# Matmul with rotary embedding: tiles in pairs over three PSUM banks, and part of the transposes on VectorE

## The chip, the cores and the metric

The kernel runs on one core of a Trainium2 chip. The metric is device time in microseconds, from launch to end of the slowest (here the only) core. Before the change five runs took 166.57 to 167.12 us, with a median of 166.95 us. A profile comes from one execution; times inside it count from its first instruction.

## The reference

`x` is 16 x 512 x 768, the weight 768 x 768, all float32; there are 12 heads of 64 columns. The product is rotated by halves of a head, with tables that depend on the row of the sequence:

```python
y = np.matmul(x, weight).reshape(batch, seq, n_heads, head_dim)
y1, y2 = y[..., :32], y[..., 32:]
out1 = y1 * cos1 - y2 * sin1
out2 = y2 * cos2 + y1 * sin2
out = concatenate([out1, out2])
```

## The kernel before, in words

The 8192 rows of `x` are 64 tiles of 128 rows. Row `4p + r` of a batch lies on partition `p` of tile `r`, so that each partition of a tile is a run of 3072 bytes in memory, and so that tile `i` needs the tables' part `i % 4`. A tile goes through these steps:

1. `load` (L75): SP's queue brings the tile to SBUF as float32 (393 KB).
2. `cast` (L86): ScalarE rounds it to float16.
3. `transpose` (L89): TensorE transposes six 128 x 128 blocks against an identity matrix into one PSUM bank (L93), and ScalarE copies them to SBUF (`xT`).
4. `mm` (L97, L103): for each of six blocks of the contraction, two matmuls, 512 and 256 columns wide, accumulate in a two-bank PSUM tile `psy`. The transposed tile is the operand that TensorE loads as weights; the weight matrix streams.
5. `rope` (L111): VectorE multiplies the product by the cosines (`tv`, L116) and, with the halves of each head swapped, by the signed sines (`qv`, L122), both out of PSUM; GpSimd adds the two (L130).
6. `store` (L136): a DMA issued from ScalarE's queue writes the tile.

The order on each engine is the order of the source, as the schedule is written by hand. In the main loop, iteration `i` loads tile `i + 5`, transposes tile `i + 1`, casts tile `i + 2`, multiplies tile `i`, rotates it, and stores tile `i - 3`. Eleven buffers hold loaded tiles, three PSUM tiles of two banks the products, and two banks the transposed blocks.

At the start the six row blocks of the weight arrive as 393 KB loads between the first tiles of `x`, VectorE rounds each (L83), and three tiles are multiplied block by block as they come. Matmuls on a zeroed tile (L141) keep TensorE busy before. The last tile is multiplied in two halves of 384 columns, each of which VectorE rotates and adds, and SP stores.

DMA issues wait in their engine's order like any other instruction: a load that waits for a buffer holds up SP alone, a store that waits holds up ScalarE's casts and copies behind it.

Of the kernel before, what the change touches and what calls it, by code (L numbers as in the profile page):

```python
# [10 lines left out]
FP32 = mybir.dt.float32  # L11
FP16 = mybir.dt.float16
MULT = mybir.AluOpType.mult
ADD = mybir.AluOpType.add


@with_exitstack
def kernel(
    ctx: ExitStack,
    tc: tile.TileContext,  # L20
    x: bass.AP,
    weight: bass.AP,
    cos: bass.AP,
    sin: bass.AP,
    n_heads: int,
    out: bass.AP,
):
    nc = tc.nc
    P = nc.NUM_PARTITIONS

    B, S, H = x.shape
    NH = int(n_heads)
    D = H // NH
    HD = D // 2
    NKT = H // P
    NMB = B * S // P
    SB = S // P
    NSPLIT = [(0, 512), (512, H - 512)]
    HALVES = [(0, H // 2), (H // 2, H // 2)]
    FIRST = 3  # L40
    AHEAD = 8


    xv = x.rearrange("b (p r) h -> b r p h", r=SB)
    ov_dram = out.rearrange("b (p r) h -> b r p h", r=SB)

    konst = ctx.enter_context(tc.tile_pool(name="konst", bufs=1))
    ident = konst.tile([P, P], FP16)
    cos_sb = konst.tile([P, SB, D], FP32)
    tee_sb = konst.tile([P, SB, D], FP32)  # L50
    w_raw = konst.tile([P, NKT, H], FP32)
    w_sb = konst.tile([P, NKT, H], FP16)

    xpool = ctx.enter_context(tc.tile_pool(name="xpool", bufs=AHEAD + 3))
    cpool = ctx.enter_context(tc.tile_pool(name="cpool", bufs=4))
    tpool = ctx.enter_context(tc.tile_pool(name="tpool", bufs=FIRST + 2))
    rpool = ctx.enter_context(tc.tile_pool(name="rpool", bufs=4))
    opool = ctx.enter_context(tc.tile_pool(name="opool", bufs=5))
    pt_pool = ctx.enter_context(tc.tile_pool(name="pt", bufs=2, space=bass.MemoryType.PSUM))
    py_pool = ctx.enter_context(tc.tile_pool(name="py", bufs=3, space=bass.MemoryType.PSUM))  # L60

    cold = konst.tile([P, 512], FP16)
    cold_ps = pt_pool.tile([P, 512], FP32, tag="pt", name="cold_ps")

    xss, x16, xTT, psys, ovs = {}, {}, {}, {}, {}

    def copy(eng, o, i_):
        if eng is nc.scalar:
            eng.copy(out=o, in_=i_)  # L69
        else:  # L70
            eng.tensor_copy(out=o, in_=i_)  # L71

    def load(i):
        xss[i] = xpool.tile([P, H], FP32, tag="xs", name="xs")
        nc.sync.dma_start(out=xss[i], in_=xv[i // SB, i % SB])  # L75

    wv = weight.rearrange("(kt p) n -> p kt n", p=P)

    def load_w(kt):
        nc.sync.dma_start(out=w_raw[:, kt], in_=wv[:, kt])  # L80

    def cast_w(kt):
        nc.vector.tensor_copy(out=w_sb[:, kt], in_=w_raw[:, kt])  # L83

    def cast(i, eng):
        x16[i] = cpool.tile([P, H], FP16, tag="xc", name="xc")  # L86
        copy(eng, x16[i], xss.pop(i))

    def transpose(i, eng):  # L89
        xc = x16.pop(i)  # L90
        pt = pt_pool.tile([P, NKT, P], FP16, tag="pt", name="pt")
        for kt in range(NKT):
            nc.tensor.transpose(pt[:, kt, :], xc[:, ts(kt, P)], ident)  # L93
        xTT[i] = tpool.tile([P, NKT, P], FP16, tag="xT", name="xT")
        copy(eng, xTT[i], pt)

    def mm(i, kt, parts=NSPLIT):  # L97
        if i not in psys:
            psys[i] = py_pool.tile([P, 2, 512], FP32, tag="psy", name="psy").rearrange(
                "p b n -> p (b n)"  # L100
            )
        for noff, nsz in parts:
            nc.tensor.matmul(  # L103
                psys[i][:, ds(noff, nsz)],
                xTT[i][:, kt, :],
                w_sb[:, kt, ds(noff % H, nsz)],
                start=(kt == 0),
                stop=(kt == NKT - 1),
            )

    def rope(i, c0, n, ps, add_eng):  # L111
        sb = i % SB
        nh = n // D
        tv = rpool.tile([P, H], FP32, tag="tv", name="tv")[:, :n]
        qv = rpool.tile([P, H], FP32, tag="qv", name="qv")[:, :n]
        nc.vector.tensor_tensor(  # L116
            out=tv.rearrange("p (h d) -> p h d", d=D),
            in0=ps.rearrange("p (h d) -> p h d", d=D),
            in1=cos_sb[:, sb, :].unsqueeze(1).broadcast_to((P, nh, D)),
            op=MULT,  # L120
        )
        nc.vector.tensor_tensor(  # L122
            out=qv.rearrange("p (h t d) -> p h t d", t=2, d=HD),
            in0=ps.rearrange("p (h t d) -> p h t d", t=2, d=HD)[:, :, ::-1, :],
            in1=tee_sb[:, sb, :].rearrange("p (t d) -> p t d", t=2)
            .unsqueeze(1).broadcast_to((P, nh, 2, HD)),
            op=MULT,
        )
        ov = ovs[i]
        add_eng.tensor_tensor(out=ov[:, ds(c0, n)], in0=tv, in1=qv, op=ADD)  # L130

    def rope_whole(i):
        ovs[i] = opool.tile([P, H], FP32, tag="ov", name="ov")
        rope(i, 0, H, psys.pop(i)[:, 0:H], nc.gpsimd)

    def store(i):  # L136
        nc.scalar.dma_start(out=ov_dram[i // SB, i % SB], in_=ovs.pop(i))

    def warm(n):
        for _ in range(n):  # L140
            nc.tensor.matmul(cold_ps, cold[:, 0:P], cold, start=True, stop=True)  # L141

    ctx.enter_context(tc.manual_schedule())

    id_dram = nc.inline_tensor(np.eye(P, dtype=np.float16), name="identity")
    nc.vector.memset(cold, 0.0)  # L146
    nc.scalar.dma_start(out=ident, in_=id_dram.ap())
    load(0)
    load_w(0)
    load_w(1)  # L150
    load(1)
    nc.scalar.dma_start(out=cos_sb, in_=cos.rearrange("(p r) d -> p r d", r=SB))
    nc.scalar.dma_start(out=tee_sb, in_=sin.rearrange("(p r) d -> p r d", r=SB))
    load_w(2)
    load_w(3)
    load(2)
    load_w(4)
    load_w(5)
    for i in range(FIRST, AHEAD):
        load(i)  # L160

    warm(9)
    cast(0, nc.vector)
    transpose(0, nc.vector)
    warm(4)
    for kt in (0, 1):
        cast_w(kt)
        mm(0, kt)
    cast(1, nc.scalar)
    transpose(1, nc.scalar)  # L170
    mm(1, 0)
    mm(1, 1)
    for kt in (2, 3):
        cast_w(kt)
        mm(0, kt)
        mm(1, kt)
    cast(2, nc.scalar)
    transpose(2, nc.scalar)
    for kt in range(4):
        mm(2, kt)  # L180
    cast_w(4)
    for i in range(FIRST):
        mm(i, 4)
    cast_w(5)
    nc.vector.tensor_scalar_mul(  # L185
        out=tee_sb[:, :, 0:HD], in0=tee_sb[:, :, 0:HD], scalar1=-1.0
    )
    cast(3, nc.scalar)
    mm(0, 5)
    rope_whole(0)  # L190
    mm(1, 5)
    rope_whole(1)
    transpose(3, nc.scalar)
    cast(4, nc.scalar)
    mm(2, 5)
    rope_whole(2)

    for i in range(FIRST, NMB):
        if i + AHEAD - FIRST < NMB:
            load(i + AHEAD - FIRST)  # L200
        if i + 1 < NMB:
            transpose(i + 1, nc.scalar)
        if 4 < i + 2 < NMB:
            cast(i + 2, nc.scalar)
        if i < NMB - 1:
            for kt in range(NKT):
                mm(i, kt)
            rope_whole(i)
            store(i - 3)
    i = NMB - 1  # L210
    ovs[i] = opool.tile([P, H], FP32, tag="ov", name="ov")
    for n, (c0, sz) in enumerate(HALVES):
        for kt in range(NKT):
            if i not in psys:
                psys[i] = py_pool.tile([P, 2, 512], FP32, tag="psy", name="psy")
            nc.tensor.matmul(  # L216
                psys[i][:, n, 0:sz],
                xTT[i][:, kt, :],
                w_sb[:, kt, ds(c0, sz)],
                start=(kt == 0),  # L220
                stop=(kt == NKT - 1),
            )
    for j in range(NMB - 4, NMB - 1):
        store(j)
    for n, (c0, sz) in enumerate(HALVES):
        rope(i, c0, sz, psys[i][:, n, 0:sz], nc.vector)
        nc.sync.dma_start(out=ov_dram[i // SB, i % SB, :, ds(c0, sz)], in_=ovs[i][:, ds(c0, sz)])


# [33 lines left out]
```

## Time and profile before

| | |
|---|---|
| median of 5 runs | 166.95 us (166.57 to 167.12) |
| the profiled execution | 166.57 us, its span 164.8 us |
| TensorE clock granted | 0.995 of full, on average |
| TensorE matmul busy | 152.6 us, 93% of the span |
| VectorE busy | 123.0 us, 75% |
| GpSimd busy | 114.5 us, 69% |
| ScalarE busy | 98.0 us, 59% |
| moved by DMA | 53.19 MB, mean 323 GB/s |

A line of the groups reads: source line, engine, operation, what it writes and reads, shape, count; then busy time in us and the mean of one in ns; then the engine's idle time ahead of such instructions and what ended it. A line of the waits reads: who waited for whom, us in total, how often, longest. A line of the chain reads: start, length, what. Rows of 40 digits or rates cut the span into equal slices. A matmul's own mean (ns) overlaps its neighbours; the pieces of the chain give the pace.

### The profile page before, as it was taken

How to read it: one execution, taken by the hardware profiler on the slowest of the kernel's cores; microseconds unless marked ns; L12 is line 12 of the kernel's file. 1: busy time of each engine (PE TensorE's matmuls, PEld its weight loads, DVE VectorE, ACT ScalarE, POOL GpSimd, SP SyncE). 2: the span in 40 equal slices, each digit the busy share in tenths (PEclk: the TensorE clock that was granted, in tenths of full speed). 3: DMA queues.
4: the chain of work that ended last, by engine and by line, in shares of the span. 5: the costliest groups of instructions: out<-in, count | busy, mean ns of one | idle time of the engine just before them, and what ended most of it. 6: DMA issues, size and time to landing. Idle time of an engine off the chain costs nothing.

```text
span 164.8 us, 3136 instructions
## 1 busy us (share of the span) xinstructions
PE 152.6 (93%) x1165; PEld 98.3 (60%) x1165; DVE 123.0 (75%) x142; ACT 98.0 (59%) x127; POOL 114.5 (69%) x67
## 2 busy tenths in 40 slices
PE   7967699999999999999999999999999999999930
PEld 2334466666666666666666666666666666666610
DVE  0532997788777787778877788777787777877792
ACT  3053666676666776667766677666776667766400
POOL 0000598778877788777887778877788777887760
PEclk9999999999999999999999999999999999999997
DMA  4999999999999999999999999999999974334535
GB/s 150 406 403 400 403 401 415 397 413 399 350 339 341 343 356 351 335 343 339 350 345 336 372 343 346 335 356 348 325 373 324 345 278 195 148 154 178 227 157 191
DMA packets 19887, 53.19 MB, mean 323 GB/s; under 512 B 2336, under 2 KB 2848, under 8 KB 19872
## 3 DMA queue, kind: packets, MB, share of 16 engines
q1 hardware_dynamic: 10368, 27.92, 49.0%
q10 hardware_dynamic: 9504, 25.07, 38.2%
q8 instruction: 9, 0.15, 0.4%
q14 instruction: 6, 0.05, 0.1%
HBM read 27.82 MB, written 25.17 MB: 322 GB/s over the span
## 4 chain that ended last, share of the span: by engine, by line
PE 88%; DMA 4%; ACT 2%; DVE 2%; issue 1%; SPq 1%; DVEq 0%
PE psy L103 74%; PE pt L93 13%; DMA xs<-in_x_dram 4%; PE psy L216 1%; DVE ov L130 1%; ACT xc L69 1%; ACT xT L69 1%; DVE qv L122 1%; SPq L80 1%; DVE tv L116 0%; SPq L75 0%; DVEq L130 0%; DVEq L116 0%
## 5 line engine op out<-in xcount | busy, mean ns | idle before, releaser
L130 POOL TENSOR_TENSOR ov<-tv,qv 128x768 f32<-128x768 f32 x63 | 114.3, 1817 | 45.1 <-DVE qv L122 43.5
L103 PE MATMUL psy<-w_sb,xT 128*128 128x512 f16 x756 | 133.5, 326 | 2.0 <-ACT xT L69 1.8
L103 PEld LDWEIGHTS <-xT 128*128 128x128 f16 x756 | 71.2, 98 | 43.5 <-ACT xT L69 2.1
L116 DVE TENSOR_TENSOR tv<-psy,cos_sb 128x768 f32<-128x768 f32 (+1 forms) x65 | 61.4, 945 | 29.9 <-PE psy L103 28.8
L69 ACT COPY xT<-pt 128x768 f16<-128x768 f16 x63 | 50.3, 798 | 49.2 <-PE pt L93 49.2
L122 DVE TENSOR_TENSOR qv<-psy,tee_sb 128x768 f32<-128x768 f32 (+1 forms) x65 | 60.8, 935 | 0.0
L69 ACT CAST xc<-xs 128x768 f16<-128x768 f32 x63 | 52.6, 836 | 5.6 <-DMA xs<-in_x_dram 5.6
L93 PE MATMUL pt<-ident,xc 128*128 128x128 f16 x384 | 32.2, 221 | 2.2 <-ACT xc L69 2.2
L93 PEld LDWEIGHTS <-xc 128*128 128x128 f16 x384 | 26.9, 99 | 11.5 <-ACT xc L69 2.9
L141 PE MATMUL cold_ps<-cold 128*128 128x512 f16 x13 | 5.3, 570 | 1.2 <-DVE cold L146 1.2
L83 DVE CAST w_sb<-w_raw 128x768 f16<-128x768 f32 x6 | 3.3, 558 | 3.8 <-DMA w_raw<-in_weight_dram 3.7
L141 PEld LDWEIGHTS <-cold 128*128 128x128 f16 x13 | 1.6, 136 | 3.5 <-issue 2.2
L71 DVE CAST xc<-xs 128x768 f16<-128x768 f32 x1 | 0.6, 559 | 3.2 <-DMA xs<-in_x_dram 3.2
L69 ACT ACT_TABLE_LOAD x1 | 1.3, 1283 | 2.1 <-issue 2.1
L216 PE MATMUL psy<-w_sb,xT 128*128 128x384 f16 x12 | 2.1, 326 | 0.0
L130 DVE TENSOR_TENSOR ov<-tv,qv 128x384 f32<-128x384 f32 x2 | 1.7, 862 | 0.1
L216 PEld LDWEIGHTS <-xT 128*128 128x128 f16 x12 | 1.2, 98 | 0.8
L71 DVE COPY xT<-pt 128x768 f16<-128x768 f16 x1 | 0.6, 557 | 0.9 <-PE pt L93 0.9
L146 DVE MEMSET cold<- 128x256 uint32 x1 | 0.3, 272 | 0.9 <-PEq L244 0.9
L244 POOL MEMSET const-float32-0.0<- 128x1 f32 x1 | 0.1, 98 | 0.2 <-issue 0.2
L185 DVE TENSOR_SCALAR tee_sb<-tee_sb 128x128 f32<-128x128 f32 x1 | 0.2, 220 | 0.0
L244 POOL MEMSET const-bfloat16-1.0<- 128x1 bf16 x1 | 0.1, 101 | 0.0
(2 smaller groups left out, 0.2 us busy)
## 6 DMA issues: line engine op xcount, KB each, us to landing
xs<-in_x_dram SPq DMA_DIRECT2D x64, 384.0 KB, 5.7
out_dram<-ov ACTq DMA_DIRECT2D x63, 384.0 KB, 4.9
w_raw<-in_weight_dram SPq DMA_DIRECT2D x6, 384.0 KB, 5.8
out_dram<-ov SPq DMA_DIRECT2D x2, 192.0 KB, 2.2
cos_sb<-in_cos_dram ACTq DMA_DIRECT2D x1, 128.0 KB, 4.7
tee_sb<-in_sin_dram ACTq DMA_DIRECT2D x1, 128.0 KB, 5.8
ident<-identity ACTq DMA_DIRECT2D x1, 32.0 KB, 3.1
```

The lines of the kernel that those rows point to most:

```text
L69: eng.copy(out=o, in_=i_)
L71: eng.tensor_copy(out=o, in_=i_)
L80: nc.sync.dma_start(out=w_raw[:, kt], in_=wv[:, kt])
L83: nc.vector.tensor_copy(out=w_sb[:, kt], in_=w_raw[:, kt])
L93: nc.tensor.transpose(pt[:, kt, :], xc[:, ts(kt, P)], ident)
L103: nc.tensor.matmul(psys[i][:, ds(noff, nsz)], xTT[i][:, kt, :], w_sb[:, kt, ds(noff % H, nsz)], start=(kt == 0), stop=(kt == NKT - 1),)
L116: nc.vector.tensor_tensor(out=tv.rearrange("p (h d) -> p h d", d=D), in0=ps.rearrange("p (h d) -> p h d", d=D), in1=cos_sb[:, sb, :].unsqu ...
L122: nc.vector.tensor_tensor(out=qv.rearrange("p (h t d) -> p h t d", t=2, d=HD), in0=ps.rearrange("p (h t d) -> p h t d", t=2, d=HD)[:, :, : ...
L130: add_eng.tensor_tensor(out=ov[:, ds(c0, n)], in0=tv, in1=qv, op=ADD)
L141: nc.tensor.matmul(cold_ps, cold[:, 0:P], cold, start=True, stop=True)
L146: nc.vector.memset(cold, 0.0)
L216: nc.tensor.matmul(psys[i][:, n, 0:sz], xTT[i][:, kt, :], w_sb[:, kt, ds(c0, sz)], start=(kt == 0), stop=(kt == NKT - 1),)
```

## The change

Tiles are handled in 32 pairs: the two tiles of pair `n` are the same part `r = n % 4` of two neighbouring batches, and so share the tables.

- **PSUM.** A pair's product lies in one tile of three banks, 1536 columns without a gap; there are two such tiles in place of three of two banks. The first tile's 768 columns are written as 512 and 256, the second's as 256 and 512. In pairs 0 and 1, where tiles are multiplied in turns, a matmul of zeros first opens the middle bank.
- **Rotation.** One VectorE multiplication takes the pair twice, once by the cosines and once by the sines with their sign and place prepared (`csn`); the swap of halves moves into GpSimd's addition, which takes 1536 columns in one instruction. A store writes a pair (786 KB).
- **Transposes.** From pair 8 on the second tile of a pair isn't transposed by TensorE. VectorE transposes 32 x 32 blocks of 4-byte words, each holding two neighbouring float16 columns. That leaves blocks in their place, so the load arranges them: four loads of 98 KB, each to 32 partitions in runs of 768 bytes, two on SP's queue and two on ScalarE's, four pairs ahead, with five buffers.
- **Column order.** A word holds two columns, so the contraction is cut as `t, e` (three parts by even and odd columns) for all tiles, and the weight's rows are loaded to match. Casts gather pairs of columns; the loads of weights on TensorE read every second float16.
- **Start.** Four tiles of `x` are loaded before the weight, the tables after it, all on SP's queue. Two tiles are multiplied with each weight block as it comes, a third one block behind.
- **End.** The six tiles of the last three pairs are multiplied into PSUM tiles of their own and rotated in two pieces each. The last tile's pieces are added by VectorE, the others by GpSimd.

```diff
-    py_pool = ctx.enter_context(tc.tile_pool(name="py", bufs=3, space=bass.MemoryType.PSUM))
+    FIRST = 8
+    AHEAD = 8
+    AHEAD_B = 4
+    ALONE = 3
+    def by_blocks(n, s):
+        return n >= FIRST and s == 1
+    xpool = ctx.enter_context(tc.tile_pool(name="xpool", bufs=FIRST + AHEAD))
+    bpool = ctx.enter_context(tc.tile_pool(name="bpool", bufs=AHEAD_B + 1))
+    rpool = ctx.enter_context(tc.tile_pool(name="rpool", bufs=3))
+    opool = ctx.enter_context(tc.tile_pool(name="opool", bufs=4))
+    py_pool = ctx.enter_context(tc.tile_pool(name="py", bufs=2, space=bass.MemoryType.PSUM))
...
+    def load_blocks(n):
+        if n >= NP or not by_blocks(n, 1):
+            return
+        b, r = where(n, 1)
+        xss[n, 1] = bpool.tile([P, H], FP32, tag="xb", name="xb")
+        src = x[b].rearrange("(j a r) (q k) -> r q a j k", r=SB, a=R, q=NQ)
+        dst = xss[n, 1].rearrange("p (j k) -> p j k", j=NQ)
+        for q in (0, 2, 1, 3):
+            eng = nc.sync if q < 2 else nc.scalar
+            eng.dma_start(out=dst[ts(q, R)], in_=src[r, q])
...
+    def cast(n, s, eng):
...
+        if by_blocks(n, s):
+            src = src.rearrange("p (j a t e) -> p t (j a) e", j=NQ, t=NT, e=2)
+        else:
+            src = src.rearrange("p (m t e) -> p t m e", t=NT, e=2)
+        copy(eng, xc.rearrange("p (t m e) -> p t m e", t=NT, e=2), src)
+    def transpose(n, s, eng):
+        xc = x16.pop((n, s)).rearrange("p (t m e) -> p t e m", t=NT, e=2)
+        pt = pt_pool.tile([P, NT, 2, P], FP16, tag="pt", name="pt")
+        for t, e in CHUNKS:
+            nc.tensor.transpose(pt[:, t, e, :], xc[:, t, e, :], ident)
...
+    def transpose_blocks(n, s):
+        xT = tpool.tile([P, NT, P, 2], FP16, tag="xT", name="xT")
+        nc.vector.transpose(
+            out=xT.bitcast(FP32).rearrange("p t m e -> p (t m e)"),
+            in_=x16.pop((n, s)).bitcast(FP32),
+        )
+        xTT[n, s] = xT.rearrange("p t m e -> p t e m")
+    def psum(n, s):
+        if n < NP - ALONE:
...
+            cut = 512 if s == 0 else 256
+            return [
+                (psys[n][:, s, ds(s * 256, cut)], 0, cut, n < 2 and s == 1),
+                (psys[n][:, s + 1, 0 : H - cut], cut, H, n < 2 and s == 0),
+            ]
...
+    def rope(n, c0, c1, ps):
...
         nc.vector.tensor_tensor(
+            out=tqs[n][:, :, c0:c1].rearrange("p j (h d) -> p j h d", d=D),
+            in0=ps.rearrange("p (h d) -> p h d", d=D)
+            .unsqueeze(1).broadcast_to((P, 2, nh, D)),
+            in1=csn[:, :, r, :].unsqueeze(2).broadcast_to((P, 2, nh, D)),
             op=MULT,
         )
+    def add(n, c0, c1, eng):
...
+            in0=tq[:, 0].rearrange("p (h t d) -> p h t d", t=2, d=HD),
+            in1=tq[:, 1].rearrange("p (h t d) -> p h t d", t=2, d=HD)[:, :, ::-1, :],
+            op=ADD,
...
+    for n in range(2, NP):
+        load_plain(n + AHEAD - 2)
+        if n + 1 < NP and by_blocks(n + 1, 1):
+            transpose_blocks(n + 1, 1)
+        for s in (0, 1):
+            for c in CHUNKS:
+                mm(n, s, *c)
+            if n < NP - ALONE:
+                prepare_b(n + 1, s)
+            prepare_a(n + 2, s)
...
+            if n >= NP - ALONE:
+                rope_alone(n, s)
+                if (n, s) != (NP - 1, 1):
+                    add(n, s * H, (s + 1) * H, nc.gpsimd)
+        if n >= 3:
+            store(n - 3, nc.scalar)
+        load_blocks(n + AHEAD_B)
+        if n < NP - ALONE:
+            rope_pair(n)
```

Here `prepare_a` casts a tile on ScalarE, and `prepare_b` transposes it on TensorE with ScalarE's copy, where it isn't one of the block tiles. At pair 28 the loop also prepares the first tiles of pairs 30 and 31.

## The prediction

> **What bounds the kernel now.** I read the chain of work that ended last first, since it alone tells what a shorter stage is worth:
>
> ```profile
> PE 88%; DMA 4%; ACT 2%; DVE 2%; issue 1%; SPq 1%; DVEq 0%
> PE psy L103 74%; PE pt L93 13%; DMA xs<-in_x_dram 4%; PE psy L216 1%; DVE ov L130 1%; ACT xc L69 1%; ACT xT L69 1%; DVE qv L122 1%; SPq L80 1%; DVE tv L116 0%; SPq L75 0%; DVEq L130 0%; DVEq L116 0%
> ```
>
> TensorE sets the pace, and 13% of the span (21.4 us) is transposes (L93). In order of time the chain is regular:
>
> ```profile
> 23.83 1.95 PE psy L103 x12
> 26.12 1.95 PE psy L103 x12
> ...
> 153.74 0.34 PE pt L93 x6
> 154.08 1.95 PE psy L103 x12
> 156.03 1.97 PE psy L216 x12
> ...
> 161.28 0.56 DVE ov L130
> ```
>
> A tile is 12 matmuls in 1.95 us and 6 transposes in 0.335 us: 2.285 us, a pair of tiles 4.57 us, with no gap from 19.1 to 158.0 us. What lies behind the last matmul is 3.8 us of VectorE and then some 3.0 us of landing and closing. Then the durations, by operation and shape:
>
> ```profile
> L130 POOL TENSOR_TENSOR ov<-tv,qv 128x768 f32<-128x768 f32 x63 | 114.3, 1817 | 45.1 <-DVE qv L122 43.5 <-POOL ov L130 1.4
> L116 DVE TENSOR_TENSOR tv<-psy,cos_sb 128x768 f32<-128x768 f32 x63 | 60.3, 957 | 29.8 <-PE psy L103 28.8 <-PE pt L93 0.9
> L69 ACT CAST xc<-xs 128x768 f16<-128x768 f32 x63 | 52.6, 836 | 5.6 <-DMA xs<-in_x_dram 5.6
> L69 ACT COPY xT<-pt 128x768 f16<-128x768 f16 x63 | 50.3, 798 | 49.2 <-PE pt L93 49.2
> L93 PE MATMUL pt<-ident,xc 128*128 128x128 f16 x384 | 32.2, 221 | 2.2 <-ACT xc L69 2.2
> L83 DVE CAST w_sb<-w_raw 128x768 f16<-128x768 f32 x6 | 3.3, 558 | 3.8 <-DMA w_raw<-in_weight_dram 3.7
> L116 DVE TENSOR_TENSOR tv<-psy,cos_sb 128x384 f32<-128x384 f32 x2 | 1.1, 552 | 0.1
> ```
>
> VectorE spends 957 + 948 ns on a tile of 2285, GpSimd 1817, ScalarE 836 + 798: all wait for TensorE. Last the transfers: their busy row stands at 9 for most of the span, which would say that they bound too, so I read the rate and the queue's own waits.
>
> ```profile
> DMA  4999999999999999999999999999999974334535
> GB/s 150 406 403 400 403 401 415 397 413 399 350 339 341 343 356 351 335 343 339 350 345 336 372 343 346 335 356 348 325 373 324 345 278 195 148 154 178 227 157 191
> ...
> SPq L75 <- ACT xc L69: 78.8, 44, 1.9
> SPq L80 <- DMA ident<-identity: 0.8, 1, 0.8
> ```
>
> Up to 40 us the loads run ahead at some 403 GB/s, and after that the rate is just what the pace asks (2 x 393 KB in 2.285 us is 344 GB/s), because SP waits for ScalarE's casts to free buffers. A queue that is never empty looks busy; it isn't full. The last line is odd: a weight load waits for the identity to land. It is the ninth transfer issued. Issues here wait for the one eight before them.
>
> **The change, by parts.** *Transposes.* 24 second tiles lose theirs on TensorE: 24 x 0.335 = 8.0 us off the path that sets the end. They lose an eviction on ScalarE too (798 ns, hidden anyway). A pair is then 2 x 1.95 + 0.335 = 4.235 us.
>
> *Block transposes on VectorE,* 128x384 as 4-byte words, are not in the trace. An element costs 1.055 ns and an instruction 0.147 us (L116's 957 and 552 for 768 and 384). The nearest rows are that 552 and L83's 558, both of 384 steps. I take 0.56; the bounds are 0.35 (two elements a step) and 0.96 (two steps an element).
>
> *The rotation.* One multiply over 2 x 1536 for a pair costs 0.147 + 3072 x 0.001055 = 3.39 us against 4 instructions, 3.81. With the transpose VectorE has 3.95 us a pair of 4.235: 93%, still behind TensorE. The transpose for pair n+2 stands behind pair n's rotation on that engine and ends some 0.3 us before pair n+1's matmuls do, a pair before it is needed. That is its cover; beyond 4.235 us the excess is paid in each of some 22 pairs.
>
> *GpSimd.* One add over 1536 takes at most 2 x 1817 = 3.63 us of 4.235. Its second input now comes with swapped halves in runs of 32, unseen on this engine: as cheap as before, or up to half dearer (5.45). I take 3.6, since L122 read such halves on VectorE for 948 against 957 ns.
>
> *PSUM.* Two buffers for pairs in place of three for tiles: pair n+2 waits for pair n's rotation, over 3.4 us into pair n+1, in time except at the start (below).
>
> *Strided operands.* Casts now gather pairs of words 24 bytes apart; ScalarE's 836 ns is kept, with twice that as the far end: 2 x 1.67 + 0.80 = 4.14, still under 4.235 (in the five plain pairs 4.94 against 4.57, +1.9 us in all). Weight loads read every second fp16. Row: 6 transposes in 0.335 us are 56 ns each, so a 128x128 load fits in 56. [...]
>
> *Transfers.* A pair now is one plain load and one 786 KB store, plus four 98 KB loads in 768-byte rows. SP issues 3 a pair (it was 2), ScalarE's queue 3 (it was 2), at some 0.34 us each beside the engine's work. On ScalarE the two small loads stand behind a store that waits for GpSimd's add of three pairs earlier, done about a pair before; behind them wait the next eviction and casts, and so TensorE. They have some 8 us until their cast. SP's half stands behind the plain load of six pairs ahead and waits there only for block buffers, when plain tiles lie far ahead. Only eight in flight means the second small load may wait for the last pair's store to land (384 KB took 4.9 us; 786 KB, some 6): about 1.5 us late, inside those 8. Demand is 1573 KB in 4.235 us, 371 GB/s. The trace has 1 KB rows at 4 to 8 us, in the stretch of the tables:
>
> ```profile
> DMA packets 773, 1.62 MB, mean 405 GB/s; under 512 B 81, under 2 KB 328, under 8 KB 773
> ...
> q10 hardware_dynamic: 279, 0.25, 18.3%
> ```
>
> Nothing was lost there. [...] The trace measured 397 to 415 with loads and stores mixed, so I take no cost; its bounds are 0 and 15 us, where 768-byte rows cost twice (1180 + 2 x 393 KB at 405: 4.85 us, +0.615 x 24).
>
> *Start.* Four tiles of x go ahead of the weights. Tiles landed 0.985 us apart from 4.38 us, so the last weights land at 4.38 + 9 x 0.985 = 13.25 (12.9 now). While they come TensorE does three tiles per chunk, 0.96 us per 0.985, from about 9.7. Cosine and sine, moved from ScalarE's queue to SP behind the weights, land near 13.9 and are hidden until pair 0 ends. I follow it, with two zeroing matmuls of 0.21: pair 0 done 15.5; pair 1, transposes between, 18.1; pair 2 wants to start at 18.45 and waits for pair 0's rotation (15.7 + 3.4), 19.1. Now the fifth tile starts at 19.1 + 2.285 = 21.4. Gain 2.3 us.
>
> *End.* Pairs 2 to 28 are 54 x 1.95 + 32 transposes x 0.335 = 116.0, so they end at 135.1. Then TensorE could do the last six in 12.4 us, but VectorE has the pair's rotation (3.4), two block transposes (1.1), six tiles in two pieces (6 x 2.0) and the last adds (some 0.7 + 0.4): 17.6, ending at 152.7. That is 5.1 us behind the last matmul, where it is 3.8 now: 1.3 lost. With 3.0 for the landing the span is 155.7.
>
> *Sum.* 164.8 - 8.0 - 2.3 + 1.3 = 155.8, the same within rounding. The profiled execution took 166.57, 1.8 over its span, which makes 157.5; the median shown stands 0.4 above it: **157.9 us**.
>
> **Rivals.** (a) *VectorE becomes the bound.* For: 93% full. Against: nothing near in the trace is slower. With 0.96 us per transpose a pair takes 4.39 at least, with gaps 4.42: 22 x 0.185 = 4.1, **162**.
>
> (b) *Transfers set the pace* in the paired stretch. [...] Against: the 1 KB rows. Milder form 4.4 us a pair, 162; at twice the price per row, **172.7**, slower than now; it turns against the change at (166.95 - 157.9)/24 = 0.38 us a pair, 341 GB/s.
>
> (c) *Strided weights load slowly.* For: two transposes stand back to back at 56 ns with no cover. [...] This is my rival on the slower side that needs a single cause: 34 tiles' transposes, decided at 9.05 us / 204 = 44 ns more per load.
>
> (d) *GpSimd becomes the bound.* It must do 29 pairs and 5 tiles, 31.5 pairs, from 19.1 on. It is hidden up to (152 - 19.1)/31.5 = 4.2 us per add; at 4.6 it ends at 164, **169**. Against: 1817 ns had 0.47 us of rest in each tile.
>
> (e) *The edit at the start or end is mis-sized,* by 2 us either way; this is in the likeliest one's own range, 155.5 to 160.5.
>
> **How the numbers follow.** Likeliest 0.62; (a) 0.10; (b) 0.13, of it half over 167; (c) 0.08; (d) 0.07. Faster: 0.62 + 0.10 + 0.05 + 0.01 = 0.78. Same, within 0.2%, which is about what a measurement of this kernel can tell: 0.03. Slower 0.19. The range leaves out the dearest of (b) and (d) and the far end below: 155.0 to 168.5.
>
> **What would show it.** Right: in the chain of waits, TensorE with pieces of 1.95 us and one 0.34 between two of them; a mean of 3.4 us for the rotation, some 0.56 for the block transpose, 3.4 to 3.6 for GpSimd's add; ScalarE and TensorE without waits for the small loads; 365 to 375 GB/s between 45 and 130 us. Wrong: TensorE waiting for VectorE's transposed tile or for a rotation in mid-span (a); casts waiting for small loads, or the rate stuck near 340 (b); six transposes in 0.6 us (c); rotations waiting for GpSimd's buffers (d).

## The result, and the profile after

The changed kernel takes 166.02 us (median of 22 executions, 164.11 to 167.72) against 166.94 for the kernel before on the same chips (43 executions). Ratios here count only fast executions, those within 1.5% of the fastest of their kernel: the ratio is 0.9894, with a 95% interval of 0.9871 to 0.9918. The change is 1.1% faster where 5.4% was predicted. Its profiled execution took 167.05 us, its span 165.2; it lies in the upper part of that range, so the losses read from it are rather large than small.

First the chain of work that ended last, by engine and by line, in the changed kernel:

```profile
DMA 49%; PE 24%; DVE 9%; ACT 8%; ACTq 4%; issue 2%; SPq 1%; DVEq 0%
DMA xb<-in_x_dram 37%; PE psy L170 21%; DVE tq L184 8%; DMA w_raw<-in_weight_dram 4%; DMA xs<-in_x_dram 4%; DMA out_dram<-ov 4%; ACT xT L77 4%; ACT xc L77 4%; PE pt L127 3%; ACTq L103 2%; ACTq L218 1%; SPq L84 1%; DVE ov L195 1%; DVE xT L134 1%; DVEq L344 0%
```

TensorE has gone from 88% of that chain to 24%, and the small loads (`xb`) hold 37%. Next the groups by form: line, engine, operation, shape and count; busy us and mean ns; idle time ahead and who ended it.

```profile
L195 POOL TENSOR_TENSOR ov<-tq 128x1536 f32<-128x1536 f32 x29 | 100.3, 3460 | 50.6 <-DVE tq L184 49.0 <-DMA out_dram<-ov 0.8 <-DMA xb<-in_x_dram 0.8
L184 DVE TENSOR_TENSOR tq<-psy,csn 128x3072 f32<-128x3072 f32 x29 | 97.4, 3358 | 24.5 <-PE psy L170 24.4
...
L77 ACT COPY xT<-pt 128x768 f16<-128x768 f16 x38 | 30.2, 798 | 56.9 <-DMA xb<-in_x_dram 30.3 <-PE pt L127 15.5 <-PE psy L170 8.7
L77 ACT CAST xc<-xb 128x768 f16<-128x768 f32 x24 | 21.7, 905 | 0.0
...
L134 DVE STREAM_TRANSPOSE xT<-xc 128x384 f32<-128x384 f32 x24 | 13.6, 568 | 0.0
```

The engines' durations are those of the prediction: the rotation 3.36 us (3.39), the block transpose 0.568 (0.56), GpSimd's add 3.46 (3.6). What is new stands in the idle column of ScalarE's copies of transposed tiles (L77, `xT`): 30.3 us of it ends with a landing of `xb`, though the copy doesn't read `xb`. It stands behind a small load's issue on ScalarE's queue. TensorE's loads of transposed tiles wait for such copies in turn:

```profile
PEld L170 <- ACT xT L77: 12.1, 17, 1.4
```

The chain in order of time (start, length, what) shows how, in the middle of the run:

```profile
53.12 0.92 ACT xc L77
54.05 0.02 issue
54.06 6.11 DMA xb<-in_x_dram
60.17 0.02 issue
60.19 5.13 DMA xb<-in_x_dram
65.32 0.02 issue
65.34 0.32 ACTq L103
...
65.75 0.80 ACT xT L77
```

A cast frees a block buffer, and SP issues a small load into it. That load lands 6.11 us later. Only then can ScalarE's queue issue a small load, which needs another 5.13 us; only then does the same queue get its next one out (ACTq L103), and the copy behind it, for which TensorE waits, can run. In the trace's semaphore events the 179 issues on SP's and ScalarE's queues share eight completion semaphores, 22 or 23 issues each, taken in turn over both queues, so that 171 issues have a predecessor on their semaphore, eight places before in the program. None of them starts before that one's landing, and 81 start within 0.06 us after it. From 48 to 118 us it is 51 of 89, among them 28 of ScalarE's 30 small loads, and seven or eight transfers are in flight for 98% of that time.

The rate per slice of the span and the landings, in us from issue, on the page:

```profile
GB/s 159 380 403 400 405 396 359 304 277 393 282 352 338 353 346 319 333 336 337 349 353 339 320 331 320 336 342 351 341 339 369 363 244 233 136 210 396 265 243 226
...
out_dram<-ov ACTq DMA_DIRECT2D x30, 768.0 KB, 6.4
xs<-in_x_dram SPq DMA_DIRECT2D x40, 384.0 KB, 6.3
xb<-in_x_dram SPq DMA_DIRECT2D x48, 96.0 KB, 5.5
xb<-in_x_dram ACTq DMA_DIRECT2D x48, 96.0 KB, 5.3
```

A load of a quarter of the size lands hardly sooner than a whole tile, and the rate stays mostly below the 371 GB/s that the full pace asks. In finer slices, from 48 to 118 us, it isn't even; the second row is the run with one load, described below:

```profile
GB/s 371 274 396 318 359 387 278 409 306 302 395 308 338 385 266 398 316 288 402 291 336 391 276 388 328 256 408 298 349 387 258 360 361 291 392 318 329 399 274 360
GB/s 374 409 404 404 384 416 414 416 374 355 418 413 417 362 390 367 420 388 404 397 348 409 327 344 404 348 406 363 380 362 388 393 348 397 346 377 363 360 325 253
```

About once a pair the change's rate falls to some 256 to 300 GB/s, with seven or eight transfers in flight. With one load it stays at 325 or more up to the last slice. SP's own waits, which before were mostly for ScalarE's casts (a free buffer), now name landings too:

```profile
SPq L103 <- ACT xc L77: 34.2, 19, 2.6
...
SPq L103 <- DMA out_dram<-ov: 12.6, 9, 6.4
SPq L103 <- DMA xb<-in_x_dram: 11.5, 15, 1.5
```

The starts of the rotations in the trace give the pace: from pair 7 (47.30 us) to pair 23 (123.29) a pair takes 4.75 us where 4.235 was predicted, 8.2 us in all. From there on, when the loads are nearly done, it is 4.235, as in these pieces of the chain:

```profile
121.23 3.90 PE psy L170 x24
125.13 0.33 PE pt L127 x6
```

So the gain of 8.0 us from the transposes is given back, inside the stretch in which it is made.

### The profile page after: what moved, and what is told of

Its sections match the earlier page's. It is cut to its first block, busy times and chain, and to the rows that moved or that the text cites. A ratio compares the mean times of both kernels' runs of the same rounds, so it can differ in the third digit from the quotient of the medians.

```text
span 165.2 us, 2658 instructions
## 1 busy us (share of the span) xinstructions
PE 148.4 (90%) x1028; PEld 89.3 (54%) x1028; DVE 128.3 (78%) x80; ACT 81.2 (49%) x101; POOL 109.4 (66%) x38
## 4 chain that ended last, share of the span: by engine, by line
DMA 49%; PE 24%; DVE 9%; ACT 8%; ACTq 4%; issue 2%; SPq 1%; DVEq 0%
DMA xb<-in_x_dram 37%; PE psy L170 21%; DVE tq L184 8%; DMA w_raw<-in_weight_dram 4%; DMA xs<-in_x_dram 4%; DMA out_dram<-ov 4%; ACT xT L77 4%; ACT xc L77 4%; PE pt L127 3%; ACTq L103 2%; ACTq L218 1%; SPq L84 1%; DVE ov L195 1%; DVE xT L134 1%; DVEq L344 0%
## 5 line engine op out<-in xcount | busy, mean ns | idle before, releaser
L195 POOL TENSOR_TENSOR ov<-tq 128x1536 f32<-128x1536 f32 (+1 forms) x34 | 109.2, 3217 | 50.6 <-DVE tq L184 49.0
L170 PE MATMUL psy<-w_sb,xT 128*128 128x512 f16 (+1 forms) x744 | 129.8, 326 | 6.0 <-ACT xT L77 5.8
L184 DVE TENSOR_TENSOR tq<-psy,csn 128x3072 f32<-128x3072 f32 (+2 forms) x37 | 104.5, 2834 | 24.5 <-PE psy L170 24.4
L77 ACT COPY xT<-pt 128x768 f16<-128x768 f16 x38 | 30.2, 798 | 56.9 <-DMA xb<-in_x_dram 30.3
L77 ACT CAST xc<-xs 128x768 f16<-128x768 f32 x38 | 34.1, 901 | 8.7 <-DMA xs<-in_x_dram 8.6
L77 ACT CAST xc<-xb 128x768 f16<-128x768 f32 x24 | 21.7, 905 | 0.0
L127 PE MATMUL pt<-ident,xc 128*128 128x128 f16 x240 | 20.0, 219 | 1.6 <-ACT xc L77 0.9
L127 PEld LDWEIGHTS <-xc 128*128 128x128 f16 x240 | 16.4, 98 | 8.6 <-ACT xc L77 2.6
L134 DVE STREAM_TRANSPOSE xT<-xc 128x384 f32<-128x384 f32 x24 | 13.6, 568 | 0.0
L170 PE MATMUL psz<-w_sb,xT 128*128 128x512 f16 (+1 forms) x24 | 4.2, 326 | 0.0
L184 DVE TENSOR_TENSOR tq<-psz,csn 128x1024 f32<-128x1024 f32 (+1 forms) x4 | 3.6, 939 | 0.0
```

Source lines behind the costliest of these rows:

```text
L127: nc.tensor.transpose(pt[:, t, e, :], xc[:, t, e, :], ident)
L134: nc.vector.transpose(out=xT.bitcast(FP32).rearrange("p t m e -> p (t m e)"), in_=x16.pop((n, s)).bitcast(FP32),)
L170: nc.tensor.matmul(ps, xTT[n, s][:, t, e, :], w_sb[:, t, e, lo:hi], start=((t, e) == CHUNKS[0] and not joined), stop=((t, e) == CHUNKS[-1] ...
L184: nc.vector.tensor_tensor(out=tqs[n][:, :, c0:c1].rearrange("p j (h d) -> p j h d", d=D), in0=ps.rearrange("p (h d) -> p h d", d=D) .unsqu ...
L195: eng.tensor_tensor(out=ovs[n][:, ds(c0, w)].rearrange("p (h t d) -> p h t d", t=2, d=HD), in0=tq[:, 0].rearrange("p (h t d) -> p h t d", ...
```

## The experiments

The pace of each run below is read from the starts of the rotations (line L184 in the change); full pace is 4.235 us for a pair with a block tile and 4.57 for one without.

**One plain load in place of the four small ones.** Does the work on the engines alone give the predicted time?

```diff
-        for q in (0, 2, 1, 3):
-            eng = nc.sync if q < 2 else nc.scalar
-            eng.dma_start(out=dst[ts(q, R)], in_=src[r, q])
+        nc.sync.dma_start(
+            out=xss[n, 1], in_=x[b].rearrange("(p r) h -> r p h", r=SB)[r]
+        )
```

> The block tile comes with one plain load of 393 KB on SP in place of four small ones: three transfers a pair in place of six, and none of them small. The block tiles hold the rows in plain order, so their part of the product is another one; VectorE's block transposes stay. Theories A and B both: TensorE sets the pace at 4.235 us a pair, pair 28 ends near 135.6 us, 16.4 us of VectorE behind it and 4 of landing, some 158 us. If something else than transfers held the pace (VectorE's queue, PSUM's two buffers), the pace stays near 4.7 and the time near 165.

158.2 us (157.99 to 158.44), ratio 0.9489 (0.9474 to 0.9504), span 156.6. Every pair from 8 to 28 takes 4.23 or 4.24 us. Its chain by engine:

```profile
PE 80%; DVE 11%; DMA 3%; ACT 2%; issue 1%; DVEq 0%; ACTq 0%
```

And its stretch from 48 to 118 us: length, then busy us and count of PE, PEld, DVE, ACT and POOL, then the clock, the share of the DMA engines and GB/s:

```profile
48.00:118.00 70.00, 70.00 (x500) 44.45 (x499) 63.73 (x33) 39.31 (x50) 56.71 (x17) 1.00 1.00 379
```

TensorE is busy for all of the 70 us, and the same bytes pass at 379 GB/s. In the change that stretch reads 65.90 us and 339 GB/s. None of this run's 47 issues in the stretch starts at the landing eight places before, and 4.4 transfers are in flight on average where the change has 7.5. So neither VectorE, GpSimd nor the strided operands hold the changed kernel, and plain loads bring its bytes fast enough: the loss comes with the four small loads. This run and the next three leave out the arrangement of blocks that the block transpose needs, so the block tiles' part of their product is another one; they tell times only.

**The same bytes in rows of 768 bytes, in one transfer.** Short rows, or the number of transfers?

```diff
+        buf = bpool.tile([P, NQ, H // NQ + 8], FP32, tag="xb", name="xb")
+        xss[n, 1] = buf[:, :, 0 : H // NQ]
+        src = x[b].rearrange("(p r) (q k) -> r p q k", r=SB, q=NQ)
+        nc.sync.dma_start(out=xss[n, 1], in_=src[r])
...
```

> The second tile of a pair comes in one transfer of 393 KB to all 128 partitions on SyncE's queue, as in the run with one plain load, but in rows of 768 bytes instead of 3072; the tile in the buffer is padded so that the rows stay apart. What is transposed is not the reference's tile, so this kernel's output differs from it; all the work on the engines is there. Theory N (the number of transfers, each issue of which waits for the landing eight places before it): three transfers a pair as there, so 158.2 us and a pace of 4.235 us a pair. Theory R (rows of 768 bytes cost each transfer time): 163 to 168 us, as the run with four such loads to all partitions (167.5).

158.23 us (157.74 to 158.39), ratio 0.9441 (0.9377 to 0.9505), pace 4.23 or 4.24 from pair 8 on, 380 GB/s from 48 to 118 us, again with no issue at such a landing. In one transfer, rows of 768 bytes cost nothing in this kernel (158.23 us beside 158.2).

**Four small loads in wide rows,** to 32 partitions each:

```diff
-        src = x[b].rearrange("(j a r) (q k) -> r q a j k", r=SB, a=R, q=NQ)
-        dst = xss[n, 1].rearrange("p (j k) -> p j k", j=NQ)
+        src = x[b].rearrange("(q a r) h -> r q a h", r=SB, a=R)
+        dst = xss[n, 1]
```

> Still four loads of 98 KB to 32 partitions each on two queues, but each row is 3072 bytes in one piece in place of four of 768; the block tiles then hold the rows in plain order, so that the block tiles' part of the product is another one. Theory A: the number of transfers is what counts, pace of a pair near 4.7 us, 164.5 to 166.5 us. Theory B by row size: pace 4.24 to 4.4, 157 to 161 us. Theory B by 32 partitions: as theory A, no change.

164.24 us (162.92 to 164.65), ratio 0.9837 (0.9786 to 0.9889), an interval that meets that of the change; pairs of up to 5.75 us. **Four small loads to all 128 partitions,** in rows of 768 bytes:

```diff
-        src = x[b].rearrange("(j a r) (q k) -> r q a j k", r=SB, a=R, q=NQ)
+        src = x[b].rearrange("(p r) (q k) -> r q p k", r=SB, q=NQ)
...
-            eng.dma_start(out=dst[ts(q, R)], in_=src[r, q])
+            eng.dma_start(out=dst[:, q], in_=src[r, q])
```

> Four loads of 98 KB per block tile in 768-byte rows, on the same two queues and at the same places as in the change, but each goes to all 128 partitions (a quarter of the columns of each row) instead of 32. The block tiles then hold the rows in plain order, so that their part of the product is another one. Number, size and row length of the transfers are those of the change; only the partitions aimed at differ. If the 32 partitions are what slows the transfers (the version with one load for four pairs ran at 180 to 217 GB/s while such a load was in flight): pace 4.24 to 4.4 us, 158 to 160.5 us. If the number of transfers (theory A) or the short rows are the cause: pace near 4.7, 164.5 to 166.5 us.

167.5 us (165.5 to 168.37), with 166.74 (166.49 to 168.56) for the kernel before beside it. The small loads land in 4.0 to 4.3 us here, sooner than the change's 5.3 to 5.5, and the time is no better. From 48 to 118 us all 30 of ScalarE's small loads start within 0.06 us of the landing eight places before, and none of SP's 45 loads: here ScalarE's queue alone is late. The rate dips as in the change (from 60 to 80 us to 157 GB/s in slices of half a microsecond, where the run with one load in short rows has 309 at least), so the dips don't need loads to 32 partitions. Neither wide rows nor all partitions bring the missing 8 us while there are four transfers; one transfer brings them even in short rows. The four stood on two queues, though, and the one on SP's. The next run puts all four on SP's, to 32 partitions; four to all partitions on SP's queue alone were not run.

**All small loads on SP's queue.** Is it that ScalarE's evictions stand behind two issues?

```diff
-            eng = nc.sync if q < 2 else nc.scalar
+            eng = nc.sync
```

> All four small loads of a tile are issued by SP, none by ScalarE. Same number of transfers, same bytes, same 768-byte rows. Theory A (an issue waits until the transfer eight before it has landed, and on ScalarE that wait holds up the evictions behind it): ScalarE's evictions no longer wait for landings of small loads (30 us of waits now, under 8 then), the pair's pace from 45 to 118 us falls from 4.74 to between 4.24 and 4.5, time 158 to 162 us. Theory B (768-byte rows, or loads aimed at 32 partitions, make the transfers themselves the limit): the pace stays near 4.7, time 165 to 167. Theory C (small loads issued too close to use): no change either, 165 to 167, with waits at the casts.

165.94 us (164.84 to 167.21), ratio 0.9936 (0.9879 to 0.9993). Moving the issues helps at first: full pace up to pair 19, at 97.8 us. Then it is 4.35 to 6.4. The waits of this run by engine, those of SP's queue, and its chain near 100 us:

```profile
ACT xT L77 <- PE pt L127: 28.4, 26, 2.4
ACT xc L77 <- DMA xb<-in_x_dram: 27.0, 13, 4.0
```

```profile
SPq L103 <- DMA out_dram<-ov: 33.5, 19, 3.5
```

```profile
96.25 6.31 DMA out_dram<-ov
102.56 0.02 issue
102.58 3.26 DMA xb<-in_x_dram
105.84 0.02 issue
105.86 0.04 ACTq L77
...
105.96 6.24 DMA out_dram<-ov
```

The evictions wait for TensorE again, as they should. Now SP is late: a small load waits for a store eight places before it to land (6.31 us), lands itself (3.26), is cast, and only then ScalarE reaches the next store but one. This ring takes 9.71 us (96.25 to 105.96) for two pairs, 4.85 a pair, and that is the pace there. The lead of four pairs hid it for the first half of the run only. So theory A foresaw rightly that the evictions would stop waiting for small loads, and wrongly the time. The time is the one that theories B and C gave, with C's waits at the casts; short rows are ruled out by the run above. Want of lead isn't what the trace shows, as the issues are late for landings, but a longer lead on SP's queue alone was not run (the one below has two queues). The queue that the issues stand on is one part and the number of places another; what share the 32 partitions have in this run isn't shown.

**Seven transfers a pair,** the plain load cut in two of 64 partitions:

```diff
-        nc.sync.dma_start(
-            out=xss[n, s], in_=x[b].rearrange("(p r) h -> r p h", r=SB)[r]
-        )
+        src = x[b].rearrange("(p r) h -> r p h", r=SB)[r]
+        for h in ((0, 64), (64, P)) if n >= FIRST else ((0, P),):
+            nc.sync.dma_start(out=xss[n, s][h[0] : h[1]], in_=src[h[0] : h[1]])
```

> As changed, but from pair 8 on the plain load of a pair is issued as two loads of 64 partitions: seven transfers a pair in place of six, the same bytes and rows. Theory A: the pace grows about with the number, 4.74 x 7/6 = 5.5 us a pair in the stretch of the waits, 172 to 180 us. Theories B and C: no change, 165 to 167.5 us.

174.45 us (173.78 to 175.68), ratio 1.0447 (1.0369 to 1.0526): one transfer more costs 8.4 us over the change, as theory A gave it, but not at the pace it gave. From pair 9 to pair 24 a pair takes 4.83 us and not 5.5 (4.73 in the change, from pair 9 to 23); 5.5 of the 8.4 us are lost in pairs 7 to 9, where SP's loads still run ahead. That the halves reach fewer partitions is in it too, and this run doesn't part the two.

**Earlier issue,** six pairs ahead with seven buffers:

```diff
-    AHEAD_B = 4
+    AHEAD_B = 6
```

> Small loads are issued six pairs ahead with seven buffers in place of four with five. Theory A: the evictions wait for the issue and not for the data, so nothing changes: 165 to 167 us. Theory C (too close to use): the lead of two more pairs takes the waits away, 158 to 161 us.

170.61 us (169.82 to 171.33), ratio 1.0224 (1.0152 to 1.0295). The pace in the middle stays at some 4.6, and a new gap of 9.05 us opens between pairs 6 and 7. It isn't the lead that was too short.

**Fewer and larger loads:** the same 32 partitions, but one load of 393 KB serves four pairs; three transfers a pair, all on SP. The lead, the buffers and the order in which VectorE writes its transpose change with it (874 ns in place of 568).

```diff
-        for q in (0, 2, 1, 3):
-            eng = nc.sync if q < 2 else nc.scalar
-            eng.dma_start(out=dst[ts(q, R)], in_=src[r, q])
+        src = x[b].rearrange("(a i) (q k) -> q a i k", a=R, q=NQ)
+        dst = groups[g].rearrange("p j r k -> p (j r) k")
+        nc.sync.dma_start(out=dst[ts(q, R)], in_=src[q])
...
```

> The quarter of a block tile that goes to 32 partitions is loaded for four pairs at once: one load of 393 KB in 768-byte rows on SP in place of four of 98 KB on two queues, so that a pair has three transfers in place of six, with the same bytes, the same rows and the same 32 partitions. VectorE's block transpose writes with a stride of four words to keep the order of rows. Theory A (number of transfers, eight in flight): no waits in mid-span, 4.235 us a pair, 157.5 to 160 us. Theory B (768-byte rows or 32 partitions): pace above 4.5, 163 us or more. If VectorE's strided write is slow (over 0.8 us), the pace is VectorE's, some 4.4, and the time 161.

174.13 us (172.78 to 177.73), ratio 1.0393 (1.0289 to 1.0497). This met something else. Its rate by slices, and its landings, from the slowest of the four executions (177.73 us):

```profile
GB/s 178 346 405 399 400 394 182 189 350 403 234 196 359 402 352 199 230 402 412 268 203 309 404 356 220 196 363 408 343 181 196 393 407 189 340 114 395 270 257 241
...
out_dram<-ov ACTq DMA_DIRECT2D x30, 768.0 KB, 10.3
xs<-in_x_dram SPq DMA_DIRECT2D x40, 384.0 KB, 8.5
xb<-in_x_dram SPq DMA_DIRECT2D x24, 384.0 KB, 10.0
```

The rate falls from 400 to some 190 GB/s again and again, and stores need 10.3 us in place of 6.4. Stores and plain loads slow with it. One to three of the large loads are in flight in the dips, and between them too. The change has shorter dips of its own, to 256 GB/s, and so has the run with four loads to all partitions (to 157 GB/s in slices of half a microsecond); what brings the rate down here is not shown.

**Pairs alone:** no block tiles but in the last two pairs; the 16 buffers of plain tiles stay.

```diff
-    FIRST = 8
+    FIRST = 30
...
```

> Pairs over three banks, the new start and the six tiles alone at the end are kept, but block tiles exist in pairs 30 and 31 only (from 30 in place of 8), so nearly all transposes are TensorE's again; loads have 16 buffers as before. All theories on the transfers: no waits in mid-span, 4.57 us a pair; pair 28 ends at 19.6 + 54 x 1.95 + 55 x 0.335 = 143.3, with 16.4 of VectorE and some 4 to the end a span of 164 and 165.5 to 166.5 us. That would say that the block tiles as changed bring nothing, their 8 us of transposes being given back in waits.

165.15 us (165.06 to 165.37), ratio 0.9907 (0.9892 to 0.9923), 4.57 us a pair. All that the changed kernel gains, pairing and the new start and end give without the block tiles.

**Block tiles in every other pair,** first with the loads on two queues, then on SP's alone:

```diff
-        return n >= FIRST and s == 1
+        return n >= FIRST and s == 1 and (n % 2 == 0 or n > NP - ALONE)
```

> Block tiles in every other pair from 8 on (13 of them, with pairs 30 and 31), the other second tiles transposed by TensorE as before; all else as changed, and the whole product is computed. Whatever slows the small loads, a pair without them gives the queues time to catch up: two pairs then have 3 plain loads, 4 small ones and 2 stores. With no waits left the time is that of pairs alone, 165.15, less 11 transposed tiles at 0.335 us: 161.5; with waits of up to 0.3 us a pair in the stretch, up to 165.

172.23 us (171.0 to 172.54), ratio 1.0295 (1.0229 to 1.0362), far from the expectation. But from pair 10 (69.4 us) on the pace is full, 4.24 and 4.57 in turns; the loss lies in 33 to 69 us, while SP's loads still run ahead. The chain there:

```profile
28.98 8.94 DMA out_dram<-ov
37.92 0.02 issue
37.94 0.35 ACTq L103
...
45.91 6.80 DMA xb<-in_x_dram
52.72 0.02 issue
...
54.72 7.17 DMA xs<-in_x_dram
61.89 0.02 issue
61.91 0.35 ACTq L103
```

ScalarE's issue of a small load (ACTq L103) stands until a store or one of SP's plain loads lands, 7 to 9 us after its start, with evictions behind it. The same tiles, with the small loads on SP as well:

> Tiles transposed by blocks in every other pair alone, and all small loads on SyncE's queue, so that no eviction stands behind a transfer's issue. If what cost the run with every other pair its 11 us at 33 to 69 us is ScalarE's queue waiting for a semaphore that a load of SyncE's run-ahead holds: about 161.5 us (the run with pairing alone, 165.15, less 13 x 0.335 = 4.4, with 0.7 for a rest of stalls). If it is the small loads themselves, whoever issues them: 165 to 172 us.

161.56 us (161.48 to 161.72), ratio 0.9648 (0.9572 to 0.9724). One line of the kernel separates it from the run before, and 10.7 us. **Two pairs of three,** on SP:

```diff
-        return n >= FIRST and s == 1
+        return n >= FIRST and s == 1 and (n % 3 != 0 or n > NP - ALONE)
...
-            eng = nc.sync if q < 2 else nc.scalar
+            eng = nc.sync
```

> Tiles transposed by blocks in two pairs of three (17 tiles), all small loads on SyncE's queue: five transfers a pair on the average, between the run with every other pair (13 tiles, 161.56) and the one with every pair (24 tiles, 165.94). If SyncE's queue still keeps up: 165.15 less 17 x 0.335 = 5.7, with the 0.8 that every other pair left open, so 160.2 us. If SyncE falls behind at five transfers a pair as it did at six: 162 to 164 us, with waits of ScalarE's casts for the loads late in the run.

**160.03 us** (159.96 to 160.35), ratio 0.9545 (0.9479 to 0.9612): 4.5% faster than the kernel before and 6.0 us below the change's median, and it computes what they compute. Its waits, and its chain in the middle:

```profile
ACT xT L77 <- PE pt L127: 44.9, 42, 1.9
POOL ov L195 <- DVE tq L184: 43.1, 27, 18.6
DVE tq L184 <- PE psy L170: 20.1, 27, 1.3
```

```profile
64.03 1.95 PE psy L170 x12
65.98 0.34 PE pt L127 x6
66.31 3.90 PE psy L170 x24
70.21 0.34 PE pt L127 x6
```

ScalarE and VectorE wait for TensorE, GpSimd for VectorE, and TensorE's matmuls of the product for none. A tile's six transposes stand between pieces of 12 matmuls; where the next tile is a block tile, 24 run in 3.90 us without a break.

**What the runs say together.** If a transfer starts when the one eight places before it has landed, then at n transfers a pair a landing may take 8/n of a pair before the next issue is late. The third column is an estimate from the measured paces (a mean over pairs with and without a block tile). The landings are medians of whole runs, with the early stretch in which loads run ahead, so the comparison is a rough one:

| block tiles, queues | transfers a pair | eight places at full pace | store / plain / small land after | time |
|---|---|---|---|---|
| one load each, short rows | 3 | 11.3 us | 6.5 / 6.9 / 6.0 | 158.23 |
| every other pair, SP | 4.5 | 7.8 | 6.1 / 6.6 / 5.7 | 161.56 |
| every other pair, two queues | 4.5 | 7.8 | 5.9 / 6.6 / 6.6 and 5.4 | 172.23 |
| two of three, SP | 5 | 7.0 | 6.2 / 6.6 / 5.4 | 160.03 |
| all, SP | 6 | 5.65 | 5.4 / 6.3 / 4.5 | 165.94 |
| all, two queues (the change) | 6 | 5.65 | 6.4 / 6.3 / 5.5 and 5.3 | 166.02 |
| all, plain load in two | 7 | 4.8 | 5.8 / 5.2 / 5.1 | 174.45 |

At five transfers or fewer the medians lie within their time, at six the plain loads don't, whichever queue issues, and at seven no kind does. The time falls with the block tiles up to there (165.15 for the 2 of the pairs-alone run, then on SP's queue 161.56 and 160.03 for 13 and 17; 0.335 us each would make it 161.5 and 160.1) and rises beyond (165.94 for 24). The second effect, ScalarE's queue, comes on top, most of all where loads run ahead.

What stays open: that issues wait for landings eight places before is read off the traces, but why the landings take so long with four small loads is not. The number of semaphores was not varied. With one load 4.4 transfers in flight move 379 GB/s, with four 7.5 move 339, so the small loads also lower what the queues deliver, and a fixed price of a transfer or a lower rate beside small loads could have a share; more places alone might then bring little. Nor did a run show why the loads on two queues lose more at the start with half of the block tiles than with all of them.

## Why the prediction was wrong, and what of it was right

- *Transposes, 24 x 0.335 = 8.0 us:* right. With one load in place of four the pace is the 4.235 us of the prediction, and the time 158.2 for 157.9.
- *Block transposes, rotation, GpSimd:* right, 0.568, 3.36 and 3.46 us for 0.56, 3.39 and 3.6. The nearest rows (instructions of 384 steps at 0.55 us) priced the unseen one. Rivals (a) and (d) fall: in the run with one load TensorE's matmuls waited 0.2 us for VectorE's rotations, in all, and VectorE not at all for GpSimd. (From the terms shown, (a)'s pair is 3.39 + 0.96 = 4.35 us and not 4.39; nothing rests on it.)
- *Strided operands:* ScalarE's casts take 905 ns for 836, hidden. Strided weights cost nothing: six transposes are still 0.33 to 0.34 us in the chain, so the row held, and rival (c), with its 0.6 us for six, fell. Unpriced was VectorE's gathering cast, 953 ns; it runs twice, at the start.
- *Start and end:* right. Pair 2's rotation started at 23.91 us, by the prediction's steps at 23.67 (19.1 and one pair of 4.57). From the start of pair 28's rotation (144.46) to the span's end it was 20.7 us for 20.6, though in other parts: VectorE 16.4 for 17.6, and then 4.4 for 3.0. In the pairs-alone run start, end and its two block tiles were to bring 2.3 - 1.3 + 0.67 = 1.7 us, and brought 1.7 (166.85 to 165.15).
- *Transfers:* **the step that failed.** "Only eight in flight means the second small load may wait for the last pair's store to land (384 KB took 4.9 us; 786 KB, some 6): about 1.5 us late, inside those 8", and then "I take no cost". It saw the limit of eight, and the landing of the store (6.4 us) was sized well. What failed is the cover. The 8 us run from the issue to the small load's own cast; but the late issue stands on ScalarE's queue, and the next eviction behind it has no such lead. The prediction had named that eviction, and yet set the lateness against the cast alone. In the trace the evictions waited 30.3 us for landings of small loads, and the casts of block tiles not at all. Two more terms were left out. The wait comes in every pair and not once: six transfers with eight places let each take 5.65 us, and the median landings were 5.3 to 6.4 us. And the small loads were tacitly fast; they land in 5.4 us. Pair 28's rotation started at 144.46 us, in the run with one load at 135.93: 8.5 us is the size of this term. That it lies inside the 0 to 15 us that were given is luck, as those were worked out from the price of short rows, which is nothing here.
- *Rival (b)* named the right resource. Of its signs, the rate near 340 came true (339). Its prices didn't: short rows in one load passed at 380 GB/s over 70 us, where 371 are needed, so neither the rows nor a limit of the rate as such were dear. No run shows the 4.4 us a pair of its milder form: a pair took 4.75 us in the change, and 4.23 or 4.24 in the run with one load. "Casts waiting for small loads" was its other sign; in the change evictions waited, since ScalarE's queue was held at the issue and not at the use. In the SP-only run the casts did wait (27.0 us).

## What to carry to other kernels

Count transfers as well as bytes: divide the number in flight (here eight over both queues) by the transfers of one loop step, and compare that time with the landing times on the profile's page. Where they were about equal, here at six transfers (5.65 us, and landings of 4.5 to 6.4), the lead of four pairs only delayed the stall, in the run with the small loads on SP's queue up to 97.8 us. An issue on ScalarE's queue held that engine's work while the queue waited for a landing (30.3 us of its copies in the change), so loads that run ahead belong on a queue with nothing else behind them. And an optimization that is limited so may be worth most in part: 17 of 24 tiles, with the loads on SP's queue, gave 160.03 us where all 24 gave 165.94.

## What the hardware showed beyond what was expected

- In the change a load of 98 KB lands after 5.3 to 5.5 us beside other traffic, one of 393 KB after 6.3: size hardly counts there.
- With loads of 393 KB to 32 partitions the rate of everything fell to some 190 GB/s again and again, and stores took 10.3 us. In pieces of 98 KB it still fell to 256 GB/s about once a pair.
- Eight transfers in flight are no measure of the rate: 4.4 moved 379 GB/s with plain loads, 7.5 moved 339 with small ones.
- Weight loads that read every second float16 are as fast as packed ones: six transposes in 0.335 us both ways.
- The swap of halves, moved to GpSimd's second operand, costs nothing there: 3.46 us for 1536 columns, where the plain add took 1.817 us for 768.
